# A fifteenth pair, earlier quarter stores and later GpSimd loads in a matmul with rotary embedding

## Chip, cores and metric

The kernel runs on one core of one Trainium2 chip. The metric is device time in microseconds (us) of one execution. A core has five engines that run their own programs: TensorE (PE in the profile; its weight loads are PEld), VectorE (DVE), ScalarE (ACT), GpSimd (POOL) and SyncE (SP), which issues transfers. Transfers can also be issued by ScalarE and GpSimd; all of them run on the same 16 DMA engines. An engine's program is in order: an instruction that waits holds everything behind it on that engine.

## What is computed

```python
y = np.matmul(x, weight)                       # x: 16 x 512 x 768, weight: 768 x 768, float32
y = y.reshape(batch, seq, n_heads, head_dim)   # 12 heads of 64
y1, y2 = y[..., :32], y[..., 32:]
out1 = y1 * cos1 - y2 * sin1                   # cos, sin: 512 x 64, halves 1 and 2
out2 = y2 * cos2 + y1 * sin2
out = np.concatenate([out1, out2], axis=-1)
```

## The kernel before

**Tiles, groups, halves, pairs.** The 8192 rows of x are 64 tiles of 128 rows. Four tiles make a group (16 groups, 0 to 15; LAST is 15). A group has two halves, and a half is a pair of tiles: pair (6,0) is the first half of group 6, tiles 24 and 25. Each tile must lie transposed in SBUF, in float16, before TensorE can multiply it with the weights.

**Two ways to a transposed tile.** The ordinary way, by rows: `load` (L210) brings one tile of 384 KB, `cast` (L245) makes it float16 on ScalarE, `turn_rows` (L265) transposes it on TensorE in twelve small matmuls, and a ScalarE copy takes it from PSUM to a buffer xt. The other way, by pairs listed in `BLOCKS` (L140 to 147): `load_quarter` (L218) brings both tiles as four quarters of 192 KB, in pieces of 768 bytes, `cast_pair` (L283) casts both on ScalarE in one instruction into xd, and `turn_pair` (L291) transposes both on VectorE in one 32 x 32 block transpose into xp. Fourteen pairs go this way. Two of them, (4,1) and (6,1), are loaded by GpSimd's queue, whose transfers cast on the way into xh, so that they need no ScalarE cast; the other twelve are loaded by SyncE into a ring of three buffers xb. `EARLY` names pairs whose quarters stand in SyncE's load list at their own tile's place; those of (5,1), (7,1) and (15,1) are mixed between row loads.

**The main work.** From tile 4 on, `walk` and `both` (L347, L391) write TensorE's order. Two streams of matmuls, one for each half of the 128 rows, run side by side, the second 1024 columns behind the first. Each pair fills three PSUM banks; the other half of the group has the other three. Once a bank, or two banks, hold both streams' sums, `rope` (L430) lets VectorE multiply them with cos and sin in one instruction (L446: 128 x 1024 elements for one bank, 128 x 2048 for two), and GpSimd adds the two products (L468) into an output buffer ov, one addition of 1536 columns for each half up to (11,0), smaller ones behind that.

**The order around the change.** The loop at L704 goes tile by tile, and where a line stands in it decides its place in each engine's program. At tile i it emits matmuls (`both`), then `bturns(i + 4)` (VectorE's pair transposes), `turns` (TensorE's transposes and ScalarE's copies), `casts` (ScalarE), `pool_loads(i + P_AHEAD)` (GpSimd's load issues, with P_AHEAD 20), and then the stores of that tile. `casts` calls `pump` (L559), which lets SyncE issue the next loads while buffers are free.

**Stores.** The output of a half goes out as two quarter stores of 384 KB (`store_half`, L505), numbered n = 0 to 51 for groups 0 to 12. The table `halves` (L675 to 679) says at which tile each is emitted on ScalarE: n = 0 to 3 at tile n + 4, n = 4 and 5 at n + 5, the others at n + 6, until group 11, where two share a tile. Each store first waits until TensorE has done all that was emitted up to then (L512), its gate, and then for GpSimd's addition. The last three groups are stored by SyncE and, at the very end, ScalarE.

Of the kernel before, what the change touches and what calls it, by code (L numbers as in the profile page):

```python
# [108 lines left out]
def kernel(  # L109
# [23 lines left out]
    QB = 4  # L133
# [3 lines left out]
    LAST = NG - 1  # L137
# [4 lines left out]
        BLOCKS[g, 1] = "pool" if g % 2 == 0 and g >= 4 else "sp"  # L142
    BLOCKS[LAST, 1] = "sp"
    BLOCKS[4, 1] = "pool"
    EARLY = ((8, 0), (8, 1), (9, 1), (10, 0), (10, 1), (11, 1), (12, 1), (13, 1), (12, 0))
    for p in EARLY:
        BLOCKS[p] = "sp"

# [52 lines left out]
    def pair_of(i):  # L201
        return i // QB, (i % QB) // 2
# [15 lines left out]
    def load_quarter(gh, q):  # L218
        g, h = gh
        b, r = where(g * QB + 2 * h)  # L220
        e = BLOCKS[gh]
        src = x[b : b + 2].rearrange("b (j a r) (q k) -> r q a (b j) k", r=SB, a=R, q=NQ)
        if q == 0:
            xs[gh] = ring("xh", NBH) if e == "pool" else ring("xb", NB)
        k = xs[gh]
        name = f"xh{k}" if e == "pool" else f"xb{k}"
        buf = xh_b[k] if e == "pool" else xb_b[k]
        dst = buf.rearrange("p (j k) -> p j k", j=2 * NQ)
        do(e, lambda eng: eng.dma_start(out=dst[ts(q, R)], in_=src[r, q]),  # L229
           writes=[f"{name}q{q}"], dma=name)  # L230
# [52 lines left out]
    def cast_pair(gh, e="act"):  # L283
        k = xs[gh]
        c = ring("xd", NCP)
        xc[gh] = c
        do(e, copy(e, xd_b[c].rearrange("p (t j e) -> p t j e", t=NT, e=2),
                   xb_b[k].rearrange("p (j t e) -> p t j e", t=NT, e=2)),
           reads=[f"xb{k}q{q}" for q in range(NQ)], writes=[f"xd{c}"])
# [20 lines left out]
    def units(g):  # L310
        if g < LAST:
            at = [0, 512, 1536, 2048, 3072] if g < LAST - 3 else range(0, 3073, 512)
            if g == LAST - 3:
                at = [0, 512, 1536, 2048, 2560, 3072]
            return [(c, z, py[:, c:z], [f"ps{b}" for b in range(c // 512, z // 512)], "pool")
                    for c, z in zip(at, at[1:])]
        u = [(0, 512, py[:, 0:512], ["ps0"], "pool")]
        for e in ("hold", "pool") * 3 + ("dve", "pe", "pool", "dve"):
            b, c, w = len(u) % 8, u[-1][1], 256
            home = pt_b[b - 6] if 6 <= b else py[:, ts(b, 512)]  # L320
            u.append((c, c + w, home[:, 0:w], [f"pt{b - 6}" if 6 <= b else f"ps{b}"], e))
        return u

    def pieces(g, s):

        out_, lo = [], s * H
        for c0, c1, ps, banks, _ in units(g):
            step = 512 if len(banks) > 1 else c1 - c0
            for k, b in enumerate(banks):
                a, z = max(lo, c0 + k * step), min(lo + H, c0 + (k + 1) * step)  # L330
                if a < z:
                    out_.append((a, z, ps[:, a - c0 : z - c0], b))
        return out_

    def mm_piece(i, piece, c, start, stop, tick):
        g, s = divmod(i, QB)
        a, z, ps, bank = piece
        get, key = xT[i]
        t, h = c
        do("pe", lambda eng: eng.matmul(  # L340
            ps, get(t, h), w_sb[:, t, h, a - s * H : z - s * H], start=start, stop=stop),
            reads=[key, f"w{t}{h}"], writes=[bank], tick=tick)
# [4 lines left out]
    def walk(pair, r):  # L347

        g, h = divmod(pair, 2)
        for bank in ((0, 1, 2) if r == 0 else (2, 0, 1)):  # L350
            opens = (r == 0) == (bank < 2)
            lo = h * 1536 + bank * 512
            parts = [(lo, lo + 512)] if bank != 1 else [(lo, lo + 256), (lo + 256, lo + 512)]
            for a, z in parts:
                i = g * QB + a // H
                for c in CHUNKS:
                    yield z - a, (g, i, a, z, r, c, opens,
                                  opens and (a, c) == (lo, CHUNKS[0]),
                                  c == CHUNKS[-1], z == lo + 512)
# [18 lines left out]
    def both(upto):  # L378

        while True:  # L380
            n = [(at[r], r) for r in (0, 1) if lines[r]]
            if not n or min(n)[0] >= upto:
                return
            r = min(n)[1]
            cols, what = lines[r].pop(0)
            at[r] += cols
            one(*what)
            g = what[0]
            for u in units(g):
                k = g, u[0]  # L390
                if k not in roped and {b for b in range(u[0] // 512, u[1] // 512)} <= ready.get(g, set()):  # L391
                    roped.add(k)
                    rope(g, u)
# [146 lines left out]
    fetch, quarters = [], []  # L540
    soon = [p for p in sorted(BLOCKS) if BLOCKS[p] == "sp" and p not in EARLY]
    for i in range(QB, NTILE):
# [3 lines left out]
        if not is_block(i):  # L546
            fetch.append(i)
            for _ in range(2 if i == QB * (LAST - 1) else 1):
                if quarters:
                    fetch.append(quarters.pop(0))  # L550
        elif pair_of(i) in EARLY:
            fetch += [(pair_of(i), q) for q in ((0, 2), (1, 3))[i % 2]]
# [97 lines left out]
    def turns(upto, most=NTILE):  # L650
        while state["turn"] < min(upto, NTILE) and most > 0:
            i = state["turn"]
            state["turn"] += 1
            if not is_block(i):
                most -= 1
                (turn_rows if rows_on[0] else turn)(i, "act")

    def bturns(upto):
        while state["bturn"] < len(pairs):
            gh = pairs[state["bturn"]]  # L660
            if gh[0] * QB + 2 * gh[1] >= upto:
                return
            turn_pair(gh)
            state["bturn"] += 1

    def pool_loads(upto):
        while state["pool"] < len(pool_pairs):
            gh = pool_pairs[state["pool"]]
            if gh[0] * QB + 2 * gh[1] >= upto:
                return  # L670
            for q in (0, 2, 1, 3):
                load_quarter(gh, q)
            state["pool"] += 1

    stores, halves = {}, {}  # L675
    for n in range(4 * (LAST - 2)):
        g, (h, c) = n // 4, divmod(n % 4, 2)
        i = 6 + n - (2 if n < 4 else n < 6) if g < LAST - 4 else min(6 + n, QB * (LAST - 2) + (n - 4 * (LAST - 4)) // 2)
        halves.setdefault(i, []).append((g, 2 * h, c))
    for g in range(LAST - 2, LAST):  # L680
        for h in (0, 2):
            stores.setdefault(QB * (g + 1) + h, []).append((g, h * H, (h + 2) * H, "sp"))

    C_AHEAD, T_AHEAD, B_AHEAD, P_AHEAD = 5, 3, 4, 20
    ROWS = QB * LAST - 2

    for i in (0, 1):
# [16 lines left out]
    for i in range(QB, NTILE):  # L704
        g, s = divmod(i, QB)
        us = units(g)
        done_to = (s + 1) * H
        rows_on[0] = QB <= i <= QB * LAST
        if i == QB * (LAST - 2) + 2:
            cast_pair((LAST, 1))  # L710
            xb_used[0] += 1
        if i < ROWS:
            if s % 2 == 0:
                for r in range(2):
                    lines[r].extend(walk(i // 2, r))
            for n in range(1, 4):
                both((i - QB) * 4608 + n * 1536)
                if n == (1 if i > QB else 2):
                    turns(i + T_AHEAD, 1)
        if i == ROWS:  # L720
            both(NTILE * 4608)
        for n, p in enumerate(pieces(g, s)) if i >= ROWS else ():
            a, z, _, bank = p
            if n == 1 and i < QB * LAST:
                turns(i + T_AHEAD, 1)
            for c in CHUNKS:
                mm_piece(i, p, c, c == CHUNKS[0], c == CHUNKS[-1],
                         tick=c == CHUNKS[-1])
            for u in us:
                if u[1] == z:  # L730
                    rope(g, u)
        bturns(i + (B_AHEAD if i < QB * (LAST - 2) else 9))
        turns(i + 1 + (T_AHEAD if i > QB else 2), 1)
        casts(i + 1 + (C_AHEAD if i > QB else 4), 1 + i % 2)
        pool_loads(i + P_AHEAD)
        for q in halves.get(i, ()):
            store_half(*q, f.count["pe"])
        for q in stores.get(i, ()):
            store(*q)
        if g == LAST:  # L740
            if s == 2:
                store(g, 0, H, "sp")
            if s == 3:
                store(g, H, 2 * H, "act")
# [44 lines left out]
```

## Time and profile before

| what | value |
|---|---|
| three runs | 148.99, 149.08, 149.20 us; median 149.08 |
| profiled execution | 149.46 us, with a span of 147.7 us from first to last instruction |
| granted TensorE clock | 1.00 |
| transfers | 27.79 MB read, 25.17 MB written |

By group of instructions, in one profiled execution:

| what | engine, line | number | mean |
|---|---|---|---|
| row cast of a tile | ACT L194 | 36 | 905 ns |
| copy of a transposed tile | ACT L194 | 34 | 800 ns |
| pair cast | ACT L194 | 12 | 1630 ns |
| TensorE transposes in rows | PE L275 | 360 (12 a tile) | 190 ns each, side by side |
| pair transpose from xd | DVE L303 | 12 | 962 ns |
| multiply of one bank, two banks | DVE L446 | 27 and 17 into tq | 1212 and 2268 ns |
| addition of a half | POOL L468 | 14 from tq, 7 from w_raw | 3479 and 3478 ns |
| load issue | POOL L229 | 8 | 608 ns |

The profile comes from one execution; times in it are microseconds from its first instruction. Busy time is the time in which an engine worked on instructions. In a list in order of time, a line is a start, a length, the engine, the line of the kernel, the operation with its output and inputs, and how many instructions were merged. Brackets at its end give the idle time before it and what ended that idle time. Names ending in q (ACTq, SPq) are an engine's own issue of a transfer or its waiting, not work. The chain of work that ended last is followed back from the last instruction.

### The profile page before, as it was taken

How to read it: one execution, taken by the hardware profiler on the slowest of the kernel's cores; microseconds unless marked ns; L12 is line 12 of the kernel's file. 1: busy time of each engine (PE TensorE's matmuls, PEld its weight loads, DVE VectorE, ACT ScalarE, POOL GpSimd, SP SyncE). 2: the span in 40 equal slices, each digit the busy share in tenths (PEclk: the TensorE clock that was granted, in tenths of full speed). 3: DMA queues.
4: the chain of work that ended last, by engine and by line, in shares of the span. 5: the costliest groups of instructions: out<-in, count | busy, mean ns of one | idle time of the engine just before them, and what ended most of it. 6: DMA issues, size and time to landing. Idle time of an engine off the chain costs nothing.

```text
span 147.7 us, 4260 instructions
## 1 busy us (share of the span) xinstructions
PE 139.3 (94%) x1846; PEld 112.4 (76%) x1846; DVE 128.1 (87%) x105; ACT 76.7 (52%) x84; POOL 116.7 (79%) x64
## 2 busy tenths in 40 slices
PE   6769999999999999999999999999999999999970
PEld 2325568888888888888888888888888888765850
DVE  0344998887889999899999999999999999999990
ACT  3444698877762742638432943275444829830010
POOL 2000389999997897959788989889889999999990
PEclk9999999999999999999999999999999999999999
DMA  4999999999999999999999999999999999986585
GB/s 120 330 395 401 401 404 397 396 325 307 323 327 323 372 387 389 376 399 390 348 380 374 396 388 368 386 390 389 383 388 394 397 401 386 387 334 243 211 310 181
DMA packets 37826, 52.44 MB, mean 355 GB/s; under 512 B 4656, under 2 KB 31024, under 8 KB 37808
## 3 DMA queue, kind: packets, MB, share of 16 engines
q1 hardware_dynamic: 21200, 30.42, 57.5%
q10 hardware_dynamic: 14432, 20.97, 38.5%
q0 software_dynamic: 2176, 0.79, 4.3%
q8 instruction: 14, 0.23, 0.6%
q14 instruction: 4, 0.03, 0.1%
HBM read 27.79 MB, written 25.17 MB: 359 GB/s over the span
## 4 chain that ended last, share of the span: by engine, by line
PE 77%; DVE 10%; DMA 5%; issue 2%; POOL 2%; SPq 1%; DVEq 0%; POOLq 0%
PE py L365 68%; DVE tq L446 6%; DMA w_raw<-in_weight_dram 5%; PE py L340 5%; PE pt L275 3%; DVE w_raw L446 2%; POOL ov L468 2%; SPq L214 1%; PE pt L260 1%; SPq L236 1%; DVE ov L415 1%; DVE py L408 0%; DVE xs L408 0%; DVE w_sb L194 0%; DVEq L57 0%
## 5 line engine op out<-in xcount | busy, mean ns | idle before, releaser
L468 POOL TENSOR_TENSOR ov<-tq 128x512 f32<-128x512 f32 (+3 forms) x34 | 76.1, 2261 | 23.1 <-DVE tq L446 23.1
L446 DVE TENSOR_TENSOR tq<-py,csn 128x1024 f32<-128x1024 f32 (+2 forms) x51 | 74.3, 1491 | 3.1 <-PE py L365 2.9
L365 PE MATMUL py<-w_sb,xt 64*128 64x512 f16 (+1 forms) x672 | 63.1, 323 | 0.0
L365 PE MATMUL py<-w_sb,xp 64*128 64x256 f16 (+1 forms) x624 | 57.2, 323 | 0.0
L365 PEld LDWEIGHTS py<-w_sb,xt 64*128 64x128 f16 x672 | 47.3, 94 | 8.3 <-DVE tq L446 0.4
L365 PEld LDWEIGHTS py<-w_sb,xp 64*128 64x128 f16 x624 | 44.6, 94 | 6.7
L194 ACT COPY xt<-pt 128x768 f16<-128x768 f16 x34 | 27.1, 800 | 30.4 <-PE pt L275 29.2
L194 ACT CAST xc<-xs 128x768 f16<-128x768 f32 x36 | 32.4, 905 | 19.6 <-PE py L365 11.5
L468 POOL TENSOR_TENSOR ov<-w_raw 128x1536 f32<-128x1536 f32 (+2 forms) x15 | 35.5, 2376 | 3.0 <-DVE w_raw L446 2.9
L446 DVE TENSOR_TENSOR w_raw<-py,csn 128x1024 f32<-128x1024 f32 (+1 forms) x22 | 35.2, 1601 | 2.3 <-PE py L365 1.9
L194 ACT CAST xd<-xb 128x1536 f16<-128x1536 f32 x12 | 19.6, 1630 | 6.0 <-PE py L365 4.0
L340 PE MATMUL py<-w_sb,xt 128*128 128x256 f16 (+1 forms) x102 | 17.0, 317 | 1.4 <-DVE w_sb L194 1.1
L340 PEld LDWEIGHTS py<-w_sb,xt 128*128 128x128 f16 x102 | 9.2, 98 | 7.4 <-DVE w_sb L194 2.7
L275 PEld LDWEIGHTS pt<-ident,xc 64*128 64x128 f16 x360 | 11.6, 95 | 1.2 <-issue 0.2
L275 PE MATMUL pt<-ident,xc 64*128 64x64 f16 x360 | 11.8, 190 | 0.0
L303 DVE STREAM_TRANSPOSE xp<-xd 128x768 f32<-128x768 f32 x12 | 11.5, 962 | 0.0
L194 DVE CAST w_sb<-w_raw 128x768 f16<-128x768 f32 x6 | 3.3, 558 | 4.2 <-DMA w_raw<-in_weight_dram 4.2
L582 PE MATMUL py<-cold 128*128 128x512 f16 x12 | 4.4, 522 | 1.4 <-DVE cold L519 1.4
L194 ACT COPY ov<-py 128x256 f32<-128x256 f32 x1 | 0.4, 372 | 10.0 <-PE py L478 10.0
L194 DVE COPY xt<-pt 128x768 f16<-128x768 f16 x2 | 1.1, 558 | 4.9 <-PE pt L260 4.9
L229 POOL DMA_DIRECT2D xh<-in_x_dram x8 | 4.8, 608 | 0.0
L260 PEld LDWEIGHTS pt<-ident,xc 128*128 128x128 f16 x36 | 2.1, 98 | 2.8 <-ACT xc L194 2.0
(26 smaller groups left out, 22.9 us busy)
## 6 DMA issues: line engine op xcount, KB each, us to landing
out_dram<-ov ACTq DMA_DIRECT2D x53, 384.0 KB, 7.3
xs<-in_x_dram SPq DMA_DIRECT2D x36, 384.0 KB, 11.2
xb<-in_x_dram SPq DMA_DIRECT2D x48, 192.0 KB, 8.9
out_dram<-ov SPq DMA_DIRECT2D x4, 768.0 KB, 3.8
w_raw<-in_weight_dram SPq DMA_DIRECT2D x6, 384.0 KB, 7.5
xh<-in_x_dram POOLq DMA_DIRECT2D x8, 96.0 KB, 13.8
out_dram<-ov SPq DMA_DIRECT2D x1, 384.0 KB, 2.3
out_dram<-ov SPq DMA_DIRECT2D x3, 128.0 KB, 2.3
```

The costliest lines, as they stand in the source:

```text
L194: eng.copy(out=o, in_=i_) if e == "act" else eng.tensor_copy(out=o, in_=i_)
L214: do(e, lambda eng: eng.dma_start(out=xs_b[k], in_=x[b].rearrange("(p r) h -> r p h", r=SB)[r]), writes=[f"xs{k}"], dma=f"xs{k}")
L229: do(e, lambda eng: eng.dma_start(out=dst[ts(q, R)], in_=src[r, q]), writes=[f"{name}q{q}"], dma=name)
L236: do(e, lambda eng: eng.dma_start(out=w_raw[:, t, h], in_=wv[t, h]), writes=[f"wr{t}{h}"], dma=f"ov{t}_{1536 * (1 - h)}")
L260: do("pe", lambda eng: eng.transpose(pt[:, t, h, :], src[:, t, h, :], ident), reads=[f"xc{c}", "ident"], writes=[f"pt{k}"], tick=(t, h) == ...
L275: do("pe", lambda eng: eng.transpose(pts[r][:, t, h, :], src[rows, t, h, :], ident[rows, rows]), reads=[f"xc{c}", "ident"], writes=[f"pt{r ...
L303: do("dve", lambda eng: eng.transpose(out=dst, in_=src), reads=rd, writes=[f"xp{z}"])
L340: do("pe", lambda eng: eng.matmul(ps, get(t, h), w_sb[:, t, h, a - s * H : z - s * H], start=start, stop=stop), reads=[key, f"w{t}{h}"], w ...
L365: do("pe", lambda eng: eng.matmul(py[:, a:z], get(t, h)[rows], w_sb[rows, t, h, a - s * H : z - s * H], start=start, stop=not opens and en ...
L446: do("dve", lambda eng: eng.tensor_tensor(out=tq.rearrange("p j (h d) -> p j h d", d=D), in0=ps.rearrange("p (h d) -> p h d", d=D) .unsque ...
L468: do(adder, lambda eng: eng.tensor_tensor(out=ov_b[o][:, ds(c0, w)].rearrange("p (h t d) -> p h t d", t=2, d=HD), in0=tq[:, 0].rearrange(" ...
L582: do("pe", lambda eng: eng.matmul(py[:, ts(b, 512)], cold[:, 0:P], cold, start=True, stop=warmed[0] < WARM - 6), reads=["cold"], writes=[f ...
```

## The change

Three edits, all of order and of one list:

- Pair (6,0), tiles 24 and 25, joins `EARLY` and so `BLOCKS`: it is loaded by SyncE in quarters, cast by one pair cast and transposed on VectorE. SyncE's load list has its four quarters where the rows of tiles 24 and 25 stood, and the quarters of (7,1) move to tiles 28 to 31.
- Quarter stores: n = 0 to 5 stay at their tiles. The others come at n + 5 instead of n + 6, and near the end one tile sooner as well, but for the last two, which stay at tile 55.
- `pool_loads`: the loads of (4,1) are emitted at tile 5 instead of 4, those of (6,1) at tile 11 instead of 7.

```diff
-    EARLY = ((8, 0), (8, 1), (9, 1), (10, 0), (10, 1), (11, 1), (12, 1), (13, 1), (12, 0))
+    EARLY = ((8, 0), (8, 1), (9, 1), (10, 0), (10, 1), (11, 1), (12, 1), (13, 1), (12, 0), (6, 0))
...
-        i = 6 + n - (2 if n < 4 else n < 6) if g < LAST - 4 else min(6 + n, QB * (LAST - 2) + (n - 4 * (LAST - 4)) // 2)
+        i = 6 + n - (2 if n < 4 else 1) if g < LAST - 4 else min(5 + n, QB * (LAST - 2) + (n - 4 * (LAST - 4)) // 2)
...
-    C_AHEAD, T_AHEAD, B_AHEAD, P_AHEAD = 5, 3, 4, 20
+    C_AHEAD, T_AHEAD, B_AHEAD = 5, 3, 4
...
-        pool_loads(i + P_AHEAD)
+        pool_loads(i + (14 if i < 11 else 16))
```

## The prediction

> **What bounds the kernel now.** I read the page's busy times first, then the chain of work that ended last, then each engine in order of time. The page gives busy time, share of the span and instructions:
>
> ```profile
> PE 139.3 (94%) x1846; PEld 112.4 (76%) x1846; DVE 128.1 (87%) x105; ACT 76.7 (52%) x84; POOL 116.7 (79%) x64
> DMA  4999999999999999999999999999999999986585
> PE 77%; DVE 10%; DMA 5%; issue 2%; POOL 2%; SPq 1%; DVEq 0%; POOLq 0%
> ```
>
> Only ScalarE has room. The DMA engines are full from 8 us to about 128 us. The chain names TensorE, so I looked there next (the chain from 46 to 70 us; start, length, what):
>
> ```profile
> 50.84 5.82 PE py L365 x53
> 56.66 0.15 PE pt L275 x9
> ...
> 56.87 1.89 PE py L365 x18
> 58.76 0.18 PE pt L275 x10
> ...
> 58.99 5.82 PE py L365 x53
> 64.81 0.15 PE pt L275 x9
> ```
>
> There is no hole between these pieces. A pair of tiles that is transposed on TensorE has two turns (L275) inside its period. By the gates that the stores wait on, pair (5,0) starts at 52.75, (5,1) at 56.65, (6,0) at 60.90 and (6,1) at 64.80. Periods are 3.90 us without turns and 4.25 us with them.
>
> VectorE in order of time (start, length, then the idle before it):
>
> ```profile
> 56.24 3.41 DVE L446 TENSOR_TENSOR tq<-py,csn 128x1024 f32<-128x1024 f32 x2
> 60.18 1.23 DVE L446 TENSOR_TENSOR w_raw<-py,csn 128x1024 f32<-128x1024 f32 x1 [0.53 <-PE py L365]
> 61.32 1.24 DVE L303 STREAM_TRANSPOSE xp<-xh 128x768 f32<-128x768 f32 x1
> 62.48 2.25 DVE L446 TENSOR_TENSOR w_raw<-py,csn 128x2048 f32<-128x2048 f32 x1
> 64.65 3.42 DVE L446 TENSOR_TENSOR tq<-py,csn 128x1024 f32<-128x1024 f32 x2
> 68.33 1.23 DVE L446 TENSOR_TENSOR tq<-py,csn 128x1024 f32<-128x1024 f32 x1 [0.27 <-PE py L365]
> 69.47 0.97 DVE L303 STREAM_TRANSPOSE xp<-xd 128x768 f32<-128x768 f32 x1
> ```
>
> After 68.33 its list has no idle above 0.13 us until 143.93. So from there VectorE, too, sets the time. GpSimd joins it:
>
> ```profile
> 104.72 3.47 POOL L468 TENSOR_TENSOR ov<-tq 128x1536 f32<-128x1536 f32 x1 [0.72 <-DVE tq L446]
> 108.91 3.47 POOL L468 TENSOR_TENSOR ov<-tq 128x1536 f32<-128x1536 f32 x1 [0.71 <-DVE tq L446]
> 112.33 3.62 POOL L468 TENSOR_TENSOR ov<-w_raw 128x512 f32<-128x512 f32 x2
> ```
>
> It last waits for VectorE at 108.78 and adds without a hole until 143.66. The last store goes out at 144.06, right behind both. The end therefore moves with VectorE at 108.8 us, as long as TensorE and the loads keep up.
>
> **The pair (6,0).** It removes two casts (905 ns) and two copies (800 ns) on ScalarE and adds one pair cast (1632 ns). ScalarE has waits of 2.8 us around there, so this costs nothing. TensorE loses 24 transposes: 4.25 - 3.90 = 0.35 us, half from 56.5, half from 58.6. VectorE gains one transpose, emitted two tiles behind that of (5,1). That puts it between the two multiplies that begin at 56.24 and 57.37. From start to next start, a transpose takes 0.89 us (53.17 to 54.06), a 1024-element multiply 1.13, a 2048-element one 2.18.
>
> So the multiply of 57.37 starts at 58.26, and VectorE is free at 58.26 + 2.18 = 60.44. The old row there started at 60.18 because TensorE released it at 60.09; that is now 59.75. New start 60.44, 0.26 late. Everything up to 65.78 keeps that lag, so it is free at 65.78 + 0.26 + 2.18 = 68.22. The old row started at 68.33, released at 68.24, now about 68.0. New start 68.22: 0.11 **early**. The two idles (60.18 - 59.55 and 68.33 - 67.96, 1.00 us in all) swallow the 0.89. At 84.28 another 0.05 us of waiting for TensorE is gained. Behind it the starts follow the natural steps, so VectorE is **0.16 us early** at 108.8, and GpSimd and the end with it.
>
> TensorE cannot bring more, because it needs the PSUM banks back. A pair takes its third bank again 0.43 us (1024 columns) after the start of the pair two later. The second multiply of (5,1) now ends at 64.99, where (6,1) would want the bank at 64.80 - 0.35 + 0.43 = 64.88: a wait of some 0.15 us. At (8,1) the room is 0.19 us before the change. So the two run in lockstep, and 0.16 of the 0.35 us arrives.
>
> **GpSimd's loads.** The first pair's four issues go out one tile later in the program, but no addition is emitted between tiles 4 and 5, so their place in the queue stays. The second pair's issues (4 x 0.59 us) leave their place behind the first addition of group 1 and go behind the first of group 2. Additions (1,1) and (2,0) run earlier: (1,1) ends at 34.3 instead of 36.68. Those of (2,1) and (3,0) end some 0.65 us later (44.16 and 47.56); at 48.52 GpSimd waits for VectorE as before, so it is even again. The transfers hardly move: the first pair's last quarter lands at 41.68, and the new issues are out by 40.65. They are needed at 61.32; before, they landed by 51.85.
>
> **Stores one tile sooner.** Each store waits on ScalarE for a TensorE count and then for GpSimd's addition. I set each addition's end against the gate one tile earlier. The room is 0.4 to 1.1 us everywhere (group 1, second half, 34.3 against 36.4; group 2, second half, 44.16 against 44.62; (7,1) 84.60 against 85.02; (9,1) 100.56 against 100.97). TensorE's gates come at most 0.2 us earlier and the additions 0.1 to 0.16, so ScalarE would wait at worst a tenth of a microsecond. Behind a waiting store stand the next copy and cast; the copies have room. The waiting store frees nothing that is short. I cost this at nothing, **provided the loads stay on time**. ScalarE's tail shows how little cover they have:
>
> ```profile
> 121.77 0.92 ACT L194 CAST xc<-xs 128x768 f16<-128x768 f32 x1
> 122.58 1.63 ACT L194 CAST xd<-xb 128x1536 f16<-128x1536 f32 x1
> 123.20 0.95 ACTq L514 DMA_DIRECT2D out_dram<-ov  x2
> ```
>
> The cast at 122.58 is that of (15,1); its last quarter landed at 121.41, 1.17 us before. VectorE's transpose of it starts at 124.24, 0.03 us behind the cast, so nothing hides a late one.
>
> How late could it be? Counted from the trace's packet records, a 1536-byte store packet takes 65 ns, a 768-byte one 36, a 3072-byte one 121. One store more in flight is 256 x 65 / 16 = 1.04 us of all 16 engines; the pair is 1024 x 36 - 256 x 121 = 5.9 us, over 16 engines 0.37 us. Loads held about 0.53 of the engines from 99 to 121 us, so the upper end is 1.41 / 0.53 = 2.7 us later. The lower end is none: from 99 to 121 us store and load packets go out about one to one (2596 to 3118), so both queues have work waiting, and one more store in the queue takes no turn from a load. Against that stands 87 to 99 us, 1510 to 2808, where stores seem to go as they come. I take 0 to 1 us, nearer the rows just ahead of the cast.
>
> The Trainium skill, "DMA: Bandwidth & Descriptors", section Queues, rings and completion order, says that an engine goes round the queues that have work, packet by packet. From 53 to 60 us the trace agrees (1134 store to 1154 load packets). By that rule alone the loads would be late only by what stores take while their queue would have been empty; the sum would stay at -0.16 us if it never is, and become the late-loads rival if it often is.
>
> **Sum.** The profiled execution took 149.46 us (span 147.7). 149.46 - 0.16 = 149.30. It lies 0.38 above the median of the runs, 149.08; so the forecast is **148.92 us**, own range 148.7 to 149.1.
>
> **Rivals.**
> Late loads (slower). (15,1)'s last quarter lands more than about 1.0 us later (1.17 less what the engines gain). Above that, VectorE stands still for the rest, and then GpSimd. At 2.0 us late the cast starts at 123.4 instead of 122.4, and the time is 148.92 + 1.0 = 149.9 us; at 2.7 us, 150.6. For it: the full DMA row, and the latency from issue to landing of a pair's last quarter, which grows from 6.6 us at 68.89 to 13.1 us at 108.33. Against it: the one-to-one packets before the cast. Chance 0.28.
>
> The new pair's own load is late (slower). Its four quarters follow one another where rows of tiles 24 and 25 landed by 49.57. At 2 us each from 43.68, as the quarters before, they land at 51.7; the cast may begin until 57.37 - 1.64 = 55.7. At 3.4 us each it would land at 57.3, and VectorE would lose 1.6 - 0.1 us: 150.4 us. Chance 0.07.
>
> TensorE's whole 0.35 us arrives (faster). If the banks come back sooner than worked out, and the transpose costs VectorE less than 0.7 us because it overlaps, all engines move by 0.35: 148.73 us or a little less. For it: TensorE heads the chain with 77%. Against it: the steps of the other twelve transposes from the same buffers are all 0.88 to 0.90. Chance 0.22.
>
> Nothing arrives (GpSimd and VectorE stay where they were): 149.08 us. Chance 0.03.
>
> **Numbers.** My forecast has 0.40. About 0.2%, 0.3 us, is what a measurement can tell from no change here. Faster takes the 0.22; within 0.2% the 0.40 and the 0.03; slower 0.28 + 0.07 = 0.35. The range 148.55 to 150.1 leaves out the worst of the late loads and little below.
>
> **What would show it.** A transpose near 57.4 in VectorE's list, and no idle at 60.4 and 68.2; TensorE's turns at 56.7 and 58.8 gone; GpSimd's last wait for VectorE 0.1 to 0.2 us earlier than 108.78; store issues at the gates, one tile sooner. The cast of (15,1) would say "DMA" as its releaser if the loads are late. I am wrong if TensorE shows holes released by VectorE around 65 us of more than 0.2 us, or if ScalarE waits for loads longer than before (2.0 us for xb, 8.0 for xs).

## The result and the profile after

The changed kernel is **slower** by about 1%: the ratio to the kernel before is 1.0112, 95% interval 1.0086 to 1.0137. Over 19 runs of each the medians are 151.45 and 149.20 us; its own runs spread from 149.23 to 153.49, those of before from 148.19 to 149.81. The ratio leaves out runs more than 1.5% above a kernel's fastest, here nine of the changed kernel's 19, so it is smaller than that of the medians. Run once more beside the first experiments, the changed kernel gave 151.06 us and 1.0080 (1.0041 to 1.0119). The forecast of 148.92 us was wrong, and its range (to 150.1) too short. The profiled execution took 151.66 us, with a span of 149.9 us.

The page after: busy time of the engines, the chain by engine, and two groups with the idle time before them and what ended it.

```profile
PE 140.3 (94%) x1822; PEld 113.1 (75%) x1822; DVE 129.0 (86%) x106; ACT 75.4 (50%) x81; POOL 116.8 (78%) x64
...
PE 52%; DMA 18%; DVE 13%; SPq 8%; ACT 3%; issue 3%; ACTq 0%; DVEq 0%
...
L194 ACT CAST xd<-xb 128x1536 f16<-128x1536 f32 x13 | 21.1, 1622 | 13.9 <-DMA xb<-in_x_dram 13.9
...
L303 DVE STREAM_TRANSPOSE xp<-xd 128x768 f32<-128x768 f32 x13 | 12.5, 963 | 2.6 <-ACT xd L194 2.6
```

The pair casts before, from the list of groups by shape:

```profile
L194 ACT CAST xd<-xb 128x1536 f16<-128x1536 f32 x12 | 19.6, 1630 | 6.0 <-PE py L365 4.0 <-DMA xb<-in_x_dram 2.0
```

TensorE has 24 instructions less and VectorE one more, as the change says. New is who waits: pair casts waited 2.0 us in all for loads before, now 13.9 us, and row casts 11.4 us after 8.0; one transpose on VectorE waits 2.6 us for a pair cast. That is the sign of being wrong that the prediction named. The chain, 5% DMA before, is now 18%.

The middle went as forecast. TensorE's chain in order of time (start, length, what), then VectorE:

```profile
50.09 13.65 PE py L365 x126
63.74 0.15 PE pt L275 x9
```

```profile
55.51 1.21 DVE L446 TENSOR_TENSOR tq<-py,csn 128x1024 f32<-128x1024 f32 x1
56.64 0.96 DVE L303 STREAM_TRANSPOSE xp<-xd 128x768 f32<-128x768 f32 x1
57.52 2.26 DVE L446 TENSOR_TENSOR tq<-py,csn 128x2048 f32<-128x2048 f32 x1
59.70 1.21 DVE L446 TENSOR_TENSOR w_raw<-py,csn 128x1024 f32<-128x1024 f32 x1
...
64.16 4.54 DVE L446 TENSOR_TENSOR tq<-py,csn 128x1024 f32<-128x1024 f32 x3
68.62 0.97 DVE L303 STREAM_TRANSPOSE xp<-xd 128x768 f32<-128x768 f32 x1
```

The two turns of tiles 24 and 25 are gone from TensorE. VectorE has the new transpose at 56.64, and the list shows no idle behind it: both idles of before, 0.53 and 0.27 us, are filled. Executions differ by up to 1.5 us in when the main part starts, so I count from its first matmul (L365): 18.72 us before, 17.98 here. The transpose of (7,1) then starts 50.75 us in before (69.47) and 50.64 now, 0.11 earlier.

The loss is at the end. ScalarE, then VectorE, in order of time with the idle before each:

```profile
120.44 0.92 ACT L194 CAST xc<-xs 128x768 f16<-128x768 f32 x1 [2.43 <-DMA xs<-in_x_dram]
...
123.39 0.91 ACT L194 CAST xc<-xs 128x768 f16<-128x768 f32 x1 [1.33 <-DMA xs<-in_x_dram]
...
125.06 1.56 ACT L194 CAST xd<-xb 128x1536 f16<-128x1536 f32 x1 [0.77 <-DMA xb<-in_x_dram]
...
126.52 0.80 ACT L194 COPY xt<-pt 128x768 f16<-128x768 f16 x1
```

```profile
120.20 3.84 DVE L446 TENSOR_TENSOR w_raw<-py,csn 128x1024 f32<-128x1024 f32 x3
126.66 0.98 DVE L303 STREAM_TRANSPOSE xp<-xd 128x768 f32<-128x768 f32 x1 [2.61 <-ACT xd L194]
```

The same transpose before, without a wait:

```profile
124.24 0.98 DVE L303 STREAM_TRANSPOSE xp<-xd 128x768 f32<-128x768 f32 x1
```

Three casts in a row wait for transfers. That of (15,1) begins at 125.06 instead of 122.58, its copy behind it is late, and VectorE stands still for 2.61 us. Its last quarter landed at 125.04, against 121.41.

Two corrections to the description: `both` begins at line 378 and `rope` at line 423; and of the quarter stores near the end, n = 49 stays at its tile (54) as well as the last two.

### The profile page after: what moved, and what is told of

Read it like the earlier page. It is cut to its first block, busy times and chain, and to the rows that moved or that the text cites. A ratio compares the mean times of both kernels' runs of the same rounds, so it can differ in the third digit from the quotient of the medians.

```text
span 149.9 us, 4210 instructions
## 1 busy us (share of the span) xinstructions
PE 140.3 (94%) x1822; PEld 113.1 (75%) x1822; DVE 129.0 (86%) x106; ACT 75.4 (50%) x81; POOL 116.8 (78%) x64
## 4 chain that ended last, share of the span: by engine, by line
PE 52%; DMA 18%; DVE 13%; SPq 8%; ACT 3%; issue 3%; ACTq 0%; DVEq 0%
PE py L365 39%; DMA xb<-in_x_dram 18%; DVE tq L446 7%; PE py L340 5%; SPq L229 5%; SPq L214 4%; PE py L582 3%; ACT xd L194 2%; DVE w_raw L446 2%; PE pt L275 2%; PE pt L260 2%; ACT xt L194 1%; DVE xp L303 1%; DVE ov L415 1%; DVE py L408 0%
## 5 line engine op out<-in xcount | busy, mean ns | idle before, releaser
L365 PE MATMUL py<-w_sb,xp 64*128 64x256 f16 (+1 forms) x672 | 60.8, 323 | 0.0
L365 PE MATMUL py<-w_sb,xt 64*128 64x512 f16 (+1 forms) x624 | 58.9, 323 | 0.6 <-ACT xt L194 0.6
L365 PEld LDWEIGHTS py<-w_sb,xp 64*128 64x128 f16 x672 | 48.6, 94 | 6.7 <-DVE w_raw L446 0.2
L365 PEld LDWEIGHTS py<-w_sb,xt 64*128 64x128 f16 x624 | 43.3, 94 | 9.4 <-DVE tq L446 1.7
L194 ACT CAST xc<-xs 128x768 f16<-128x768 f32 x34 | 30.6, 906 | 22.5 <-DMA xs<-in_x_dram 11.4
L194 ACT COPY xt<-pt 128x768 f16<-128x768 f16 x32 | 25.5, 799 | 23.3 <-PE pt L275 21.3
L194 ACT CAST xd<-xb 128x1536 f16<-128x1536 f32 x13 | 21.1, 1622 | 13.9 <-DMA xb<-in_x_dram 13.9
L303 DVE STREAM_TRANSPOSE xp<-xd 128x768 f32<-128x768 f32 x13 | 12.5, 963 | 2.6 <-ACT xd L194 2.6
L582 PE MATMUL py<-cold 128*128 128x512 f16 x12 | 5.4, 623 | 1.4 <-DVE cold L519 1.4
L582 PEld LDWEIGHTS py<-cold 128*128 128x128 f16 x12 | 1.6, 144 | 3.6 <-issue 2.2
```

The costliest lines, as they stand in the source:

```text
L194: eng.copy(out=o, in_=i_) if e == "act" else eng.tensor_copy(out=o, in_=i_)
L303: do("dve", lambda eng: eng.transpose(out=dst, in_=src), reads=rd, writes=[f"xp{z}"])
L365: do("pe", lambda eng: eng.matmul(py[:, a:z], get(t, h)[rows], w_sb[rows, t, h, a - s * H : z - s * H], start=start, stop=not opens and en ...
L582: do("pe", lambda eng: eng.matmul(py[:, ts(b, 512)], cold[:, 0:P], cold, start=True, stop=warmed[0] < WARM - 6), reads=["cold"], writes=[f ...
```

## The experiments

**Theory after the result:** the DMA engines are full, the sooner stores and the pair's small packets take their time from the loads, and the loads pass the slack that (15,1) has. **Rival:** VectorE has no room for the added transpose, and TensorE loses time on PSUM banks. Each kernel was run beside the kernel before, whose medians there were 148.95 to 149.16 us; ratios are to that. Each kernel has one profiled execution, so a difference between two of them can be chance: the two of the changed kernel alone are 2.1 us apart at the last pair.

**The changed kernel again**, as a control, no edit.

> The changed kernel, unchanged, beside the kernel before on this chip. Late-loads theory: about 2 us slower (the ratio seen was 1.011), the last quarter of (15,1) lands 2 to 4 us later than in the kernel before, ScalarE waits over 10 us in all for xb, VectorE stands still at that pair's transpose for 1 to 3 us. Rival (VectorE has no room for the transpose of (6,0), and TensorE loses time on PSUM banks): the loss shows at 55 to 80 us, and little at the last pair.

Measured: 151.06 us, ratio 1.0080. In its profile ScalarE waits 8.4 us for xb, where over 10 us was expected, and VectorE stands still at (15,1):

```profile
124.99 0.98 DVE L303 STREAM_TRANSPOSE xp<-xd 128x768 f32<-128x768 f32 x1 [1.19 <-ACT xd L194]
```

From 55 to 80 us VectorE's list is as in the first profile. Counted from the first matmul of the main part, its multiplies start within 0.03 us of those of the kernel with the pair alone (below) from 3 to 104 us in, and 1.3 us later behind (15,1). In the first profile 0.7 us is lost by 104 us, and 3.4 us behind (15,1). So all or most of the loss is at the end, as the theory says. This execution took 149.99 us, less than most of the kernel's.

**Each edit undone, or alone.**

```diff
e4_pair_undone (from the changed kernel)
-    EARLY = (..., (12, 0), (6, 0))
+    EARLY = (..., (12, 0))
e6_stores_undone (from the changed kernel)
-        i = 6 + n - (2 if n < 4 else 1) if g < LAST - 4 else min(5 + n, ...
+        i = 6 + n - (2 if n < 4 else n < 6) if g < LAST - 4 else min(6 + n, ...
e1_pair_only (from the kernel before)
-    EARLY = (..., (12, 0))
+    EARLY = (..., (12, 0), (6, 0))
e2_stores_only (from the kernel before)
+        i = 6 + n - (2 if n < 4 else 1) if g < LAST - 4 else min(5 + n, ...
e3_gpsimd_loads_only (from the kernel before)
+        pool_loads(i + (14 if i < 11 else 16))
```

> The changed kernel with fourteen pairs: tiles 24 and 25 by rows again, the stores sooner and the GpSimd loads later as changed. Late-loads theory with the store as its larger part (1.04 us of all engines against 0.37): still 1 to 2 us slower than before, last quarter of (15,1) at 123 to 124.5. If the 768-byte packets of the pair are the larger part: within 0.4 us of before. Rival (no room on VectorE): the time of before, within 0.3 us, with the loads as late as they are in the changed kernel.

> The changed kernel with its quarter stores at the tiles of before; pair (6,0) and the later GpSimd loads stay. Late-loads theory with the store as its larger part: most of the loss is gone, 0.2 us faster to 0.5 us slower than before. If the pair's packets are the larger part: 1 us or more slower. Rival (no room on VectorE): as slow as the changed kernel, some 2 us.

> The kernel before with pair (6,0) alone. Late-loads theory, store as the larger part: 0.2 us faster to 0.5 us slower than before. Pair as the larger part: 1 us or more slower. Rival (no room on VectorE): some 2 us slower with no late loads.

> The kernel before with the sooner stores alone; fourteen pairs, GpSimd's loads as before. Theory (each cause of its own uses up the slack of 1.17 us in front of (15,1), and only together they pass it): within 0.3 us of before, last quarter of (15,1) 1 to 2 us later than before, counted from the first matmul of the main part. Rival (sooner stores need the later GpSimd loads, or ScalarE waits for additions): 0.5 us or more slower, with ScalarE's store issues late around 36 us.

> The kernel before with the later place of GpSimd's second loads alone. Theory: the transfers queue behind the first pair's anyway, the additions are even again by 48.5 us: within 0.2 us of before, last quarter of (15,1) within 0.5 us. If the later loads themselves take the engines at a worse moment: up to 0.5 us slower and that quarter 1 us later.

Measured, with one profiled execution of each. "Last quarter" is when that of (15,1) lands, counted from the first matmul of the main part; in the kernel before its cast was due 103.86 us in (122.58 - 18.72). The last two columns are what SyncE's and ScalarE's queues had moved 60 us in, summed from the trace's packet records.

| kernel | median us | ratio, interval | last quarter us | loads MB | stores MB |
|---|---|---|---|---|---|
| before | 149.20 | | 102.69 | 17.76 | 9.43 |
| pair | 149.10 | 0.9990, 0.9961 to 1.0020 | 102.84 | 17.77 | 9.45 |
| GpSimd loads | 149.14 | 1.0002, 0.9987 to 1.0018 | 103.12 | 17.57 | 9.51 |
| stores | 149.41 | 0.9996, 0.9971 to 1.0021 | 104.22 | 17.51 | 9.83 |
| stores, GpSimd loads | 149.38 | 1.0017, 0.9995 to 1.0039 | 103.81 | 17.51 | 9.88 |
| pair, GpSimd loads | 149.37 | 1.0000, 0.9978 to 1.0022 | 104.16 | 17.51 | 9.49 |
| all three, again | 151.06 | 1.0080, 1.0041 to 1.0119 | 104.95 | 17.27 | 9.88 |
| all three, first | 151.45 | 1.0112, 1.0086 to 1.0137 | 107.06 | 17.07 | 9.88 |

No edit alone and neither pair of edits that was run costs anything that the runs resolve; all three together cost 1%. The third pair of edits, (6,0) with the sooner stores, was not run, so it is not shown that GpSimd's later loads are needed for the loss.

The slack is 103.86 - 102.69 = 1.17 us. A kernel that stays near it pays next to nothing (VectorE's gap at (15,1) is 0.3 us with the stores alone, 0.4 with pair and GpSimd loads), one that passes it pays. How much, four profiles with all three edits and the last pair's cast at its place tell: the two in the table and those of the last two experiments below. Their last quarters come 2.26, 4.37, 3.57 and 2.94 us later than in the kernel before, and they end 0.86, 2.94, 2.18 and 1.54 us later, all counted from the first matmul of the main part. The end moves with the quarter one to one, less 1.4 us each time (1.38 to 1.43).

Which edit delays the quarter most stays open. Alone they delay it by 0.15, 0.43 and 1.53 us, and that their sum, 2.11, is about the 2.26 of the control is luck as far as the table tells, because the pairs of edits do not add up: stores and GpSimd loads are 1.12 us late together, less than the stores alone, pair and GpSimd loads 1.47 us, far more than the two. With the pair undone 1 to 2 us of loss was expected to stay, with the store as the larger part; that was **missed**, at 149.38 us. The rival's time came there, but not its late loads: the quarter was 1.1 us sooner than in the control. Undoing the stores brought the time back as expected. Either is enough. The single edits came as expected.

The rival falls with the pair alone, whose VectorE and ScalarE read:

```profile
64.19 4.55 DVE L446 TENSOR_TENSOR tq<-py,csn 128x1024 f32<-128x1024 f32 x3
68.65 0.98 DVE L303 STREAM_TRANSPOSE xp<-xd 128x768 f32<-128x768 f32 x1
```

```profile
120.82 0.90 ACT L194 CAST xc<-xs 128x768 f16<-128x768 f32 x1
121.63 1.62 ACT L194 CAST xd<-xb 128x1536 f16<-128x1536 f32 x1
```

The transpose of (7,1) starts 68.65 - 18.02 = 50.63 us in, 0.12 before its old place, and the last pair's cast has no wait before it. VectorE ends 142.97 - 18.02 = 124.95 us in, against 143.93 - 18.72 = 125.21: 0.26 us early. At the multiply for which 0.16 had been worked out (108.70 before, 107.83 here) it is 0.17 us early.

**A store taken away.** Part of the output is not written here.

```diff
-        halves.setdefault(i, []).append((g, 2 * h, c))
+        if g != 5:
+            halves.setdefault(i, []).append((g, 2 * h, c))
```

> The changed kernel without the four quarter stores of group 5, so that part of the output is not written; everything else as changed. Theory (the loads are late because the DMA engines have too much to do by then): four stores are 4.2 us of all engines, so the loads land 3 us or more earlier behind that point, no gap at (15,1), 148.5 to 149.2 us. Rival (the loss comes from the order of ScalarE's program or from VectorE's added transpose): still 150.5 to 151.5 us.

Measured: 149.14 us, ratio 1.0011 (0.9988 to 1.0034). The last quarter lands 101.99 us in, 3.0 us sooner than in the control, and 60 us in, 17.94 MB are loaded instead of 17.27; VectorE has no gap. With all three edits in place, four stores less bring the whole loss back. VectorE's added transpose is still there, so it is not the loss. The edit also takes four issues and their waits out of ScalarE's program, which was not tested apart.

**Stores the other way**, one tile later than before, pair and GpSimd loads kept.

```diff
-        i = 6 + n - (2 if n < 4 else 1) if g < LAST - 4 else min(5 + n, ...
+        i = 7 + n - (3 if n < 4 else 2 if n < 6 else 0) if g < LAST - 4 else min(7 + n, ...
```

> The changed kernel with the quarter stores from n = 6 on two tiles later than in it, so one tile later than in the kernel before; pair (6,0) and GpSimd's later loads stay. Theory: the loads get the engines' time that the stores leave, the last quarter of (15,1) lands 1 us earlier than with the stores of before, 148.6 to 149.2 us. Rival (stores have next to no part in it): like the pair with GpSimd's loads, 149.4 us, whatever the stores do. If late stores hold output buffers: slower than 149.5 us, GpSimd waiting on transfers.

Measured: 148.98 us, ratio 1.0000 (0.9980 to 1.0019); last quarter 102.23 us in, with 17.69 MB loaded and 9.09 stored at 60 us. ScalarE's and VectorE's tail:

```profile
121.22 0.90 ACT L194 CAST xc<-xs 128x768 f16<-128x768 f32 x1
122.03 1.64 ACT L194 CAST xd<-xb 128x1536 f16<-128x1536 f32 x1
```

```profile
120.01 3.82 DVE L446 TENSOR_TENSOR w_raw<-py,csn 128x1024 f32<-128x1024 f32 x3
123.75 0.97 DVE L303 STREAM_TRANSPOSE xp<-xd 128x768 f32<-128x768 f32 x1
```

Against pair and GpSimd loads with the stores of before (104.16) the quarter is 1.9 us sooner, more than the 1 us expected. The direction is the theory's, from both sides. The time is that of the kernel before: nothing waited for that quarter there.

**The last pair moved out of the way.**

```diff
-        if i == QB * (LAST - 2) + 2:
+        if i == QB * (LAST - 2) + 5:
             cast_pair((LAST, 1))
...
-        bturns(i + (B_AHEAD if i < QB * (LAST - 2) else 9))
+        bturns(i + B_AHEAD)
```

> The changed kernel with the cast of (15,1) three tiles later in ScalarE's program and its transpose five tiles later in VectorE's; all loads and stores as changed. Theory (loads late, and the loss is the wait at that pair, which also holds up the copies behind it on ScalarE): the loads land as late as before this edit, but VectorE's gap of 1 to 3 us goes, and 1 to 2 us of the loss with it: 149.0 to 149.9 us. Rival (the loss is spread over TensorE and VectorE from the middle on): still 150.5 to 151.5 us.

> The kernel before with the later cast and transpose of (15,1) alone, as a control of that edit. Theory: the cast had 1.17 us of slack and the transpose started 0.03 us behind it, so there is next to nothing to win: 148.8 to 149.3 us. If that pair holds up the kernel before as well in many executions: 0.3 us or more faster.

Measured: 150.49 us, ratio 1.0085 (1.0053 to 1.0116), on the changed kernel; the same edit on the kernel before 149.39 us, 1.0023 (1.0001 to 1.0046), just above the 149.3 expected. The theory's 149.0 to 149.9 was **missed**, and the time is at the edge of its rival's. But the loss is not spread from the middle on: VectorE's multiplies are within 0.02 us of those with the pair alone from 3 to 100 us into the main part, and 2.2 us late from 117 us on. The gap at the transpose is gone, but the rows behind that pair are as late. ScalarE and VectorE of the edited changed kernel:

```profile
122.79 0.92 ACT L194 CAST xc<-xs 128x768 f16<-128x768 f32 x1 [0.82 <-DMA xs<-in_x_dram]
...
125.69 0.91 ACT L194 CAST xc<-xs 128x768 f16<-128x768 f32 x1 [1.27 <-DMA xs<-in_x_dram]
...
126.49 0.81 ACT L194 COPY xt<-pt 128x768 f16<-128x768 f16 x1
```

```profile
124.43 3.49 DVE L446 TENSOR_TENSOR tq<-py,csn 128x1024 f32<-128x1024 f32 x3 [0.41 <-PE py L365]
128.90 3.49 DVE L446 TENSOR_TENSOR tq<-py,csn 128x1024 f32<-128x1024 f32 x3 [0.98 <-PE py L365]
```

A row cast waits until its load lands at 125.66, its copy ends at 127.30, TensorE's next transposes wait for that (its PSUM buffer) and VectorE then for TensorE. So the loss is not the wait at one pair; (15,1) is only where it shows first. Whatever is cast last waits for the loads.

**Quarter of the last partitions first**, and **four buffers**.

```diff
e8_quarter3_first (from the changed kernel)
-        ... for q in (0, 2, 1, 3)]
+        ... for q in (3, 0, 2, 1)]
-            fetch += [(pair_of(i), q) for q in ((0, 2), (1, 3))[i % 2]]
+            fetch += [(pair_of(i), q) for q in ((3, 0), (2, 1))[i % 2]]
-                if j[1] == 0:
+                if j[1] == 3:
-        if q == 0:
+        if q == (0 if e == "pool" else 3):
e10_four_xb_buffers (from the changed kernel)
-    NX, NB, NBH, NC, NCP, NXT, NXP, NOV = 10, 3, 3, 5, 2, 8, 4, 4
+    NX, NB, NBH, NC, NCP, NXT, NXP, NOV = 9, 4, 2, 5, 2, 8, 4, 4
```

> The changed kernel with the quarter of partitions 96 to 127 issued first in each pair, then 0, 2, 1. In all profiles that quarter, issued last, lands 1.5 to 4.5 us behind the third. If it is late because it is the last of the four: the quarter now last lands as late, and the time stays near 151 us. If that quarter itself is slow: it lands no later than the other three, the pair is complete 1 to 3 us sooner, VectorE's gap goes, 149.0 to 149.8 us.

> The changed kernel with four buffers xb instead of three (two xh instead of three and nine xs instead of ten pay for it), so that SyncE may issue a pair's quarters one cast earlier. Theory (total work of the DMA engines is short, and stores take what loads do not ask for): 0.5 to 1.5 us of the loss comes back where loads had run dry, 149.5 to 150.5 us. If only the buffers make the loads late: 149.0 us or less. If nothing but the engines' total work counts: 151 us as before.

Measured: 150.82 us, ratio 1.0117 (1.0076 to 1.0158), and 151.09 us, 1.0132 (1.0107 to 1.0157): neither helps. With quarter 3 first, the pair is complete 106.25 us in, between the 104.95 and 107.06 of the old order, and VectorE still stands still for 1.45 us. So it is not the quarter of the last partitions that holds the pair up. Which of the four lands last the trace does not tell: all four add to one counter (`dma=name` in `load_quarter`), 64 steps a pair, and a landing is read as every sixteenth step. With four buffers 0.5 to 1.5 us was expected to come back; that was **missed**, and the time is the 151 us written down for the case that only the engines' total work counts. The buffer was paid for with a row buffer and one of GpSimd's, so it tells only that buffers were not what the changed kernel lacked most.

## Why the prediction was wrong, point by point

**Pair (6,0): right.** TensorE's turns went, VectorE's two idles swallowed the transpose, (7,1) was 0.11 us early in the changed kernel, and the pair alone is 0.17 us early on VectorE where 0.16 had been worked out, and ends 0.26 us early. The runs cannot resolve that: 0.9990, with an interval of 0.3% to either side.

**GpSimd's loads: half wrong.** "The transfers hardly move" was the step. The last of them landed at 51.85 us before and at 55.9 with this edit alone, 53.1 and 53.9 in the changed kernel's profiles. That is in time for 61.32, but SyncE's queue had moved 0.19 MB less 60 us in, and (15,1) came 0.43 us later in the one profile. I had costed nothing.

**Stores, and the lateness of the loads: wrong, and this decided.** The stores went out at their gates, 1.8 to 2.5 us sooner, as said, up to n = 35; behind that, in the changed kernel, late casts on ScalarE hold some of them back. The failed step is the size of the loads' lateness: "I take 0 to 1 us, nearer the rows just ahead of the cast", which the sum took as nothing. The runs show 2.26 and 4.37 us with all three edits, against a slack of 1.17. The about one-to-one packets from 99 to 121 us (2696 store to 3118 load packets; 2596 in the prediction is a slip) say nothing of the stretches before; by then the deficit had long been there. Already 60 us in, stores are 0.40 to 0.45 MB ahead wherever they are issued sooner, which is one quarter store, and loads 0.25 MB behind with the stores alone, 0.49 and 0.69 MB with all edits. It is hardly made up: 100 us in, 0.27, 0.38 and 0.73 MB are still missing. The stores are not the only cause: pair and GpSimd loads leave the loads 0.25 MB behind as well. A better guide than the turn-taking in one stretch would have been the sum of work, one store's 1.04 us and the pair's 0.37 us, over the loads' share: the 2.7 us that the prediction set as its upper end lies between the two profiles. That the sum is the right rule is argued, since the single edits do not add up to it.

The Trainium skill, "DMA: Bandwidth & Descriptors", section Queues, rings and completion order, has the engines take turns among the queues with work. By that rule sooner stores harm loads where the store queue would otherwise be empty. The runs do not speak against it: from 40 to 48 us into the main part the kernel before sends 1018 store to 1475 load packets, not one to one, and the sooner stores alone make it 1196 to 1388. When an engine's store queue was empty no run tells.

**The late-loads rival: the right mechanism, with too small a chance (0.28).** Its price was nearly right: it put 2.0 us of lateness at 1.0 us of time, and the line through the four profiles, lateness less 1.4 us, makes it 0.6. What it had too small is the lateness: its upper end of 2.7 us was passed in the first profile. One reason can be seen and was not tested by itself: in the changed kernel's first profile ScalarE waits nine times for a pair's load, each late pair cast frees its buffer xb late, and SyncE's next issues wait for that, so lateness may feed itself. That would also fit the wide spread of its runs; that a fourth buffer did not help speaks rather against it.

**The other rivals.** The new pair's own load was in time: its cast began at 51.32, 0.24 us late, and its transpose ran at 56.64 without a wait. TensorE's whole 0.35 us did not arrive, even with the pair alone: VectorE ended 0.26 us early there.

## What to carry to other kernels

Where the DMA engines are full nearly from end to end, as here, a transfer that is moved ahead can be paid for by one behind it: estimate what each edit adds, and set it against the smallest slack of any load, at the far end of the kernel, not where the edit is made. Slack is shared: three edits that each cost nothing alone can pass it together, so test the edits of such a change in combination and singly. And a store that nobody waits for need not go sooner: with stores later than in the kernel before, the changed kernel took the time of before, and its last quarter had 0.46 us more room (one profile).

## What the runs showed that I had not expected

The main part starts 17.66 to 19.12 us into the span, from one execution to the next of kernels that are alike up to there. That is up to 1% of the time, more than most edits here, so places are compared from the first matmul of the main part, and ratios need many runs.

The last part of a pair's load takes longest. Of the 64 counter steps of (15,1) in the kernel before, the 16th, 32nd and 48th came at 111.22, 113.78 and 116.47 us, the 64th at 121.41. Nor do loads land strictly in the order of their issue: (7,1), whose last quarter was issued at 41.97, was complete at 57.46, when the pair issued behind it, from 43.10 on, had made sixteen steps already (57.07). With the quarters in another order the last sixteen steps still take longest; why it is so stays open.
